# Layer 1's position bias prepared in layer 0's up stage instead of its down stage, and a cast of the down stage put behind three copies

## The chip, the cores and the metric

The kernel runs on one core of a Trainium2 chip. The metric is the device time of one launch in microseconds (us), as the median of several runs; lower is better. A hardware profile of one execution shows when each engine worked: TensorE (PE, with its weight loads PEld), VectorE (DVE), ScalarE (ACT), GpSimd (POOL), and the queues from which SyncE (SP), ACT and POOL issue transfers.

## The reference

One inference step of a two-layer encoder over 1024 new frames and 8 running streams of 16 frames, all in float32. Layer 0 uses sliding-window attention with a distance penalty, layer 1 attention over 9 chunks of 64 with a learned bias per head on the clipped relative distance. Behind each attention comes a squared-ReLU MLP:

```python
def relpos_bias(q_pos, k_pos, table):          # layer 1 only; table is rel_bias_b[0], 16 heads x 257
    rel = jnp.clip(q_pos[:, None] - k_pos[None, :], -MAX_REL, MAX_REL) + MAX_REL
    bias = table.astype(jnp.float32)[:, rel]
    return jnp.where(band_mask(q_pos, k_pos, LEFT_CHUNKS_B)[None], bias, NEG)

def mlp(x, g_norm, w_up, w_down):              # 1024 -> 4096 -> 1024
    return jnp.square(jax.nn.relu(rmsnorm(x, g_norm) @ w_up)) @ w_down
```

## The kernel before

Each layer runs four stages one after the other: attention, the output projection, the **up stage** (`mlp_up`) and the **down stage** (`mlp_down`). Every float32 operand is split into a high part (a cast, on ACT, line 128) and a low part (source minus high, on DVE, line 134), and every product of two tiles is three matmuls (`mm3`, lines 745 to 747).

The up stage walks over 16 blocks `b` of 256 hidden columns. `weights(b)` loads two raw tiles `ru` through SP's queue (three buffers), forms differences on DVE and splits them into `wq` and `w`. `tokens` runs seven products per block into the PSUM tiles `ps_x`, `ps_y`, `ps_z`; ACT copies or activates them (lines 866, 871, 875, 818, 819) and DVE adds them (868, 877, 886) into the tiles `h` (seven buffers, taken in turn). Block 0 does this in two halves of 256 tokens. POOL then stores sums of `h` to DRAM (`hd`, line 910).

The down stage multiplies in 40 products per layer, two rounds of 20 (`RANK`). Product `n` needs one tile `a` of rows (768 KB, loaded from `hd` through SP's queue, line 1026, three buffers, loaded as soon as the product that used the buffer is done) and one weight tile `w` (from the raw tiles `r`, or from their sum `s`, line 1062). Both are split first: `split_h` and `split_w`. A product is three groups of 12 matmuls, one for each of three PSUM banks `ps_c`. Products come in chains that go on accumulating into the same three banks; between two products of a chain some outputs read the banks, either as a copy to `o` by ACT (line 1165), or as an addition into `x` by DVE (line 1177). The copies `o` are added to DRAM by POOL's transfers.

In layer 0's down stage two functions prepare the bias of layer 1. `prep_bias`, ahead of product 20, loads the table `tb`, fills `fr` and `big` on DVE, turns the table into `fr`, writes it to DRAM (`fd`) and repeats it there 128 times (`rd`, 3 MB). `spread_bias`, ahead of product 24, reads 16 pieces of `rd` into `big` and stores that to DRAM (`biasSd`). All 20 transfers go through SP's queue, at places that `self.behind` (an order without a semaphore) sets behind the loads issued so far.

The order on each engine is set by a scheduler that simulates the program, by the hand-set orders of `self.behind`, `self.follow` (TensorE) and `chain` (DVE), and by priorities.

Of the kernel before, what the change touches and what calls it, by code (L numbers as in the profile page):

```python
# [8 lines left out]
F32 = mybir.dt.float32  # L9
F32R = mybir.dt.float32r  # L10
AF = mybir.ActivationFunctionType
ALU = mybir.AluOpType
# [4 lines left out]
P = 128  # L17
# [5 lines left out]
H = 16  # L23
KV = 4
G = 4
# [5 lines left out]
RANK = 20  # L31
# [21 lines left out]
BIG = 1e30  # L53
NREL = 257
# [40 lines left out]
class Build:  # L95
# [681 lines left out]
    def mlp_up(self, layer, sx, x8, rp, raw0):  # L777
        nc = self.nc
        tt = nc.vector.tensor_tensor
        with ExitStack() as st:  # L780
# [113 lines left out]
            self.pe = None  # L894
            for b in range(NFB):
                quad, ws = weights(b)
                eh = [hp.tile([P, 3 * 3 * P], F32, tag="h", name="h", bufs=7) for _ in range(2)]
                if b == 0:
                    tokens(eh, quad, ws, slice(0, 256), False)
                    tokens(eh, quad, ws, slice(256, 512), True)  # L900
                else:
                    tokens(eh, quad, ws, slice(0, 512), True)
                if b % 2 == 0:
                    even = eh
                    self.forms_even(b // 2, eh)
                else:
                    self.forms_odd(b // 2, even + eh, hp.tile([P, 3 * 3 * P], F32, tag="h", name="ht", bufs=7))
# [59 lines left out]
    def mlp_down(self, layer, out):  # L967
# [3 lines left out]
        with ExitStack() as st:  # L971
# [15 lines left out]
            for n, tags in enumerate(DOWN_HOME):  # L987
                pool = self.pool(st, f"d{n}_{layer}")
                for t in tags.split():
                    if t == "bias":  # L990
                        self.bias_tiles(pool)
                        pool.tile([P, 248], F32, tag="pad", name="pad")
                    elif t[0] == "+":
                        pool.tile([P, int(t[1:])], F32, tag="gap", name="gap")
                    else:
                        homes[t] = pool
                        slots[t] = fresh(t)
# [71 lines left out]
            def split_h(n):  # L1069
                if n < total:  # L1070
                    a = aa[n]
                    low[n] = [self.split(a[:, 0], a[:, 1], a[:, 1].bitcast(F32))[1]]

            low, total_of = {}, {}
            banks = None
# [48 lines left out]
                    chain(z)  # L1124
            late = iter(self.late)
            for n, (s, p, g, first, final, reads, _) in enumerate(seq):
                if layer == 0 and n == RANK:
                    self.prep_bias(self.dp)
                if layer == 0 and n == RANK + 4:
                    self.spread_bias(self.dp)  # L1130
                if n + AHEAD < total:
                    load_w(n + AHEAD)
                split_h(n + 1)
# [17 lines left out]
                for i in range(3):  # L1151
                    if i == 2 and n + 2 in total_of:
                        chain(total_of[n + 2])
                    c = slice(i * P, i * P + P)
                    z = [
                        self.mm3(
                            banks[i], a[:, 0, k, c], a[:, 1, k, c], w[:, 0, k], w[:, 1, k],
                            first and k == 0, k == 3,
                        )
                        for k in range(4)  # L1160
                    ]
                    self.follow(z[0][0], z[-1][1])
                    for o, v in reads:
                        if o in adds:
                            nc.scalar.activation(adds[o][i], banks[i], AF.Copy, scale=float(v))  # L1165
# [11 lines left out]
                        chain(tt(x, x, banks[i], ALU.add if v > 0 else ALU.subtract))  # L1177
                    for o in {o // 2: o for o, _ in reads if left[o] == n}.values():
                        store_x(o, PARTS[o // 2][i])
# [10 lines left out]
                            break  # L1190
                        load_h(m)

    def bias_tiles(self, pool):
        self.tb = pool.tile([H, NREL], F32, tag="tb", name="tb")
        self.fr = pool.tile([H, 384], F32, tag="fr", name="fr")
        self.big = pool.tile([P, KV, 288], F32, tag="big", name="big")

    def prep_bias(self, dp):
        nc = self.nc
        with ExitStack() as st:  # L1200
            tb, fr, big = self.tb, self.fr, self.big
            a = nc.sync.dma_start(tb, self.ins["rel_bias_b"][0])
            self.behind(self.sp, a)
            self.behind(self.dve, nc.vector.memset(fr, 0.0))
            self.behind(self.dve, nc.vector.memset(big, BIG))
            nc.vector.tensor_scalar(
                fr[:, 127:383], tb[:, 256:0:-1], -1.0, tb[:, 256:257], ALU.mult, ALU.add
            )
            fd = dp.tile([H, 384], F32, tag="fd", name="fd")
            nc.sync.dma_start(fd, fr)  # L1210
            rd = dp.tile([H, P, 384], F32, tag="rd", name="rd")
            nc.sync.dma_start(rd, fd[0:H].unsqueeze(1).to_broadcast([H, P, 384]))
            ra = rd[0:H]

            def fsrc(h, off, n, nh, hs, w):
                return bass.AP(
                    tensor=ra.tensor, offset=ra.offset + h * P * 384 + 127 + off,
                    ap=[[383, n], [hs * P * 384, nh], [1, w]],
                )

            self.fsrc = fsrc

    def spread_bias(self, dp):
        nc, big, fsrc = self.nc, self.big, self.fsrc
        for h4 in range(G):
            for b in range(2):
                r = slice(h4 * 32 + b * 16, h4 * 32 + b * 16 + 16)
                c = 256 + b * 16
                for z in (
                    nc.sync.dma_start(big[r, :, b * P : b * P + P], fsrc(h4, 0, 16, KV, G, P)),  # L1230
                    nc.sync.dma_start(big[r, :, c : c + 16], fsrc(h4, P, 16, KV, G, 16)),
                ):
                    self.behind(self.sp, z)
        self.biasSd = dp.tile([KV, P, 288], F32, tag="biasSd", name="biasSd")
        nc.sync.dma_start(self.biasSd[0:KV].rearrange("j p c -> p j c"), big)

    def prep_gains(self):
        nc, I = self.nc, self.ins
# [593 lines left out]
def make_plan(tail, second):  # L1832
# [16 lines left out]
AFTER = mybir.DependencyInfo(mybir.DependencyClass.NoSync, mybir.DependencyReason.DATA)  # L1849
EARLY = (300, 150, 110, 90)  # L1850
DOWN_HOME = (
    "s1", "r0", "o0", "+512", "s0", "o1", "+512", "r3", "x5", "x6", "x7", "bias", "r4", "r5", "+384", "x8", "x0", "x2", "+640",
    "a0", "x1", "x3", "x4", "r6", "a1", "a2", "w0", "w1", "r7", "r8", "r9", "r10",
)
TAIL = 6
# [56 lines left out]
```

## Time and profile before

| | |
|---|---|
| runs | 2354.15, 2354.36, 2357.34 us; median 2354.36 us |
| span of the profiled execution, first to last instruction | 2349.6 us (its own time is not given beside it) |
| TensorE busy | 2273.2 us, 97% of the span |
| DVE, ACT, POOL busy | 73%, 57%, 27% |
| layer 0's up stage, about | 426 to 798 us |
| layer 0's down stage, about | 798 to 1133 us |
| layer 1's up stage, about | 1655 to 2017 us |
| layer 1's down stage, about | 2017 to 2346 us |

In lines of the timeline the first number is the start in us from the start of the span, the second the duration in us; then come engine, line, operation, output<-input with shape and type, and in brackets the idle time of the engine ahead of it and what ended it. A row `SPq` or `POOLq` is the issue of a transfer, not the transfer. In tables of waits the three numbers are the sum in us, how often, and the longest. In tables of windows the columns are the stretch, its length, the busy time (and count) of PE, PEld, DVE, ACT and POOL, the granted TensorE clock, the busy share of the DMA engines and GB/s.

### The profile page before, as it was taken

To read this page: it belongs to the slowest core of one execution; us is meant where nothing else is said; L and a number is where in the kernel's file an instruction comes from. 1 tells how busy PE (TensorE), PEld (TensorE's weight loads), DVE (VectorE), ACT (ScalarE), POOL (GpSimd) and SP (SyncE) were. 2 spreads that over 40 slices of the span, in tenths; PEclk is the share of its full clock that TensorE was granted. 3 is DMA by queue.
4 is the path that set the end of the run, shared out by engine and by line. 5 is a ranking of instruction groups with operands and counts; after the bars stand their busy time and mean duration, and the time that the engine had idled before them with its cause. 6 is when DMAs were issued, how large, how long until landed. Compare 5 with 4: busy or idle time off the path is not lost.

```text
span 2349.6 us, 33397 instructions
## 1 busy us (share of the span) xinstructions
PE 2273.2 (97%) x11429; PEld 1899.3 (81%) x11429; DVE 1718.3 (73%) x3075; ACT 1332.0 (57%) x2684; POOL 644.7 (27%) x950
## 2 busy tenths in 40 slices
PE   8999999899999999999899899999899999999999
PEld 6787877788888888778778778887888888888887
DVE  6888786766656578898577776877666566678987
ACT  3777674555555555344377666665655555555443
POOL 4434332313213111002433444345132132210011
PEclk9999999999999999999999999999999999999999
DMA  7435546234334687848654656555243343877567
GB/s 262 128 103 177 166 141 208 89 122 162 132 112 152 218 231 174 272 142 206 191 157 114 190 151 180 166 172 186 72 162 132 114 160 113 276 212 197 183 165 198
DMA packets 226715, 392.70 MB, mean 167 GB/s; under 512 B 51592, under 2 KB 126288, under 8 KB 226448
## 3 DMA queue, kind: packets, MB, share of 16 engines
q1 hardware_dynamic: 188816, 283.58, 37.8%
q0 software_dynamic: 36432, 102.26, 16.0%
q10 hardware_dynamic: 1296, 4.72, 0.5%
q8 instruction: 90, 1.47, 0.3%
q14 instruction: 81, 0.66, 0.1%
HBM read 236.51 MB, written 156.85 MB: 167 GB/s over the span
## 4 chain that ended last, share of the span: by engine, by line
PE 73%; DVE 11%; DMA 8%; ACT 3%; issue 2%; POOL 2%; SPq 1%; ACTq 0%; DVEq 0%; POOLq 0%
PE ps_c L745 7%; PE ps_c L746 7%; PE ps_c L747 7%; PE ps_x L745 5%; PE ps_x L747 5%; PE ps_x L746 5%; PE ps_mm L219 3%; PE ps_mm L221 3%; PE ps_mm L220 3%; PE ps_y L747 2%; PE ps_y L746 2%; PE ps_y L745 2%; PE ps_tr L326 2%; DMA a<-hd 2%; DVE w L134 1%
## 5 line engine op out<-in xcount | busy, mean ns | idle before, releaser
L746 PE MATMUL ps_c<-w,a 128*128 128x512 f32 x960 | 374.0, 390 | 3.9 <-DVE w L134 3.9
L745 PE MATMUL ps_c<-w,a 128*128 128x512 f32 x960 | 374.1, 390 | 3.2 <-ACT o L1165 1.7
L747 PE MATMUL ps_c<-w,a 128*128 128x512 f32 x960 | 373.5, 389 | 0.0
L910 POOL DMA_DIRECT2D hd<-h x272 | 149.4, 552 | 594.3 <-ACT h L819 378.4
L745 PEld LDWEIGHTS ps_c<-w,a 128*128 128x128 f32 x960 | 180.2, 188 | 42.9 <-issue 2.7
L746 PEld LDWEIGHTS ps_c<-w,a 128*128 128x128 f32 x960 | 180.2, 188 | 42.7 <-DVE w L134 5.6
L747 PEld LDWEIGHTS ps_c<-w,a 128*128 128x128 f32 x960 | 180.2, 188 | 37.4
L128 ACT CAST a<-a 128x1536 fp32r<-128x1536 f32 x80 | 118.6, 1483 | 154.6 <-DMA a<-hd 154.6
L219 PE MATMUL ps_mm<-w,hh 128*128 128x512 f32 x432 | 173.9, 403 | 12.8 <-ACT hh L128 5.4
L221 PE MATMUL ps_mm<-w,hl 128*128 128x512 f32 x432 | 172.4, 399 | 1.4 <-DVE hl L134 1.2
L220 PE MATMUL ps_mm<-w,hh 128*128 128x512 f32 x432 | 171.4, 397 | 0.3
L134 DVE TENSOR_TENSOR a<-a 128x1536 fp32r<-128x1536 f32 x80 | 140.6, 1757 | 40.6 <-ACT a L128 40.5
L745 PE MATMUL ps_x<-sx,w 128*128 128x512 f32 (+1 forms) x408 | 157.8, 387 | 4.5 <-ACT h L866 2.7
L128 ACT CAST w<-ru 128x512 fp32r<-128x512 f32 (+1 forms) x160 | 109.9, 708 | 84.4 <-PE ps_y L746 32.0
L128 ACT CAST w<-s 128x2048 fp32r<-128x2048 f32 x56 | 107.1, 1912 | 88.2 <-DVE s L1062 78.8
L747 PE MATMUL ps_x<-sx,w 128*128 128x512 f32 (+1 forms) x408 | 154.2, 378 | 0.3 <-DVE w L134 0.3
L746 PE MATMUL ps_x<-sx,w 128*128 128x512 f32 (+1 forms) x408 | 154.1, 378 | 0.0
L134 DVE TENSOR_TENSOR w<-s,w 128x2048 fp32r<-128x2048 f32 x56 | 128.2, 2289 | 32.3 <-ACT w L128 32.0
L1182 POOL DMA_DIRECT2D xp<-o x28 | 36.2, 1294 | 411.6 <-ACT o L1165 391.0
L134 DVE TENSOR_TENSOR w<-ru,w 128x512 fp32r<-128x512 f32 (+1 forms) x160 | 129.7, 813 | 14.8 <-ACT w L128 14.7
L134 DVE TENSOR_TENSOR ptl<-ps_tr,pth 128x512 fp32r<-128x512 f32 x180 | 122.5, 685 | 21.2 <-ACT pth L128 17.5
L818 ACT ACTIVATE h<-h 128x512 f32<-128x512 f32 (+1 forms) x102 | 61.9, 607 | 122.1 <-DVE h L868 93.0
(274 smaller groups left out, 6152.9 us busy)
## 6 DMA issues: line engine op xcount, KB each, us to landing
a<-hd SPq DMA_DIRECT2D x80, 768.0 KB, 6.2
hd<-h POOLq DMA_DIRECT2D x272, 192.0 KB, 2.5
ru<-in_w_up SPq DMA_DIRECT2D x64, 512.0 KB, 3.9
r<-in_w_down SPq DMA_DIRECT2D x32, 1024.0 KB, 9.8
xp<-o POOLq DMA_DIRECT2D x28, 768.0 KB, 9.5
o<-oTd SPq DMA_DIRECT2D x50, 256.0 KB, 3.9
x<-xp SPq DMA_DIRECT2D x23, 512.0 KB, 5.5
xp<-xo SPq DMA_DIRECT2D x18, 512.0 KB, 2.9
```

Of the source, the lines that this page charges most:

```text
L128: a = nc.scalar.copy(hi, src)
L134: return a, e.tensor_tensor(lo, src, hi.bitcast(F32), ALU.subtract)
L219: nc.tensor.matmul(ps, a, w[:, 0, k, :], start=(k == 0), stop=False)
L220: nc.tensor.matmul(ps, a, w[:, 1, k, :], start=False, stop=False)
L221: self.lp = nc.tensor.matmul(ps, b, w[:, 0, k, :], start=False, stop=(k == KC - 1))
L326: self.lp = nc.tensor.transpose(pt[:, i, :], get(i), self.ident)
L745: a = mm(ps, ah, bh, start=first, stop=False, skip_group_check=True)
L746: mm(ps, ah, bl, start=False, stop=False, skip_group_check=True)
L747: return a, mm(ps, al, bh, start=False, stop=last, skip_group_check=True)
L818: a = nc.scalar.activation(t, src, AF.Relu)
L910: return lambda p, z: self.nc.gpsimd.dma_start(self.hd[c // 4][:, p, c % 4], z)
L1182: nc.gpsimd.dma_start(dst, z, accum_op=ALU.add)
```

## The change

The bias of layer 1 is now prepared in layer 0's up stage, between `weights(0)` and the first block's products, in one function. Its two tiles are the first two buffers of `h`: `part` holds `tb` and `fr`, and `big` the 16 pieces. All its transfers but one are issued by POOL; `rd` is still issued by SP. In the down stage of both layers the place of the bias tiles is left as a gap of the same size, and the cast of product 2's rows is ordered behind the last of the copies `o` that read product 0's banks (`self.copied`).

```diff
@@ mlp_up
                 quad, ws = weights(b)
+                if layer == 0 and b == 0:
+                    part, big = [hp.tile([P, 3 * 3 * P], F32, tag="h", name="hb", bufs=7) for _ in range(2)]
+                    self.spread_bias(self.dp, part, big)
                 eh = [hp.tile([P, 3 * 3 * P], F32, tag="h", name="h", bufs=7) for _ in range(2)]
@@ mlp_down
-                    low[n] = [self.split(a[:, 0], a[:, 1], a[:, 1].bitcast(F32))[1]]
+                    z = self.split(a[:, 0], a[:, 1], a[:, 1].bitcast(F32))
+                    if n == 2:
+                        self.behind(self.copied, z[0])
+                    low[n] = [z[1]]
...
-                if layer == 0 and n == RANK:
-                    self.prep_bias(self.dp)
-                if layer == 0 and n == RANK + 4:
-                    self.spread_bias(self.dp)
...
-                            nc.scalar.activation(adds[o][i], banks[i], AF.Copy, scale=float(v))
+                            self.copied = nc.scalar.activation(
+                                adds[o][i], banks[i], AF.Copy, scale=float(v)
+                            )
@@ bias
-    def bias_tiles(self, pool):
...
-    def prep_bias(self, dp):
...
+    def spread_bias(self, dp, part, big):
+        nc = self.nc
+        dma = nc.gpsimd.dma_start
+        tb, fr = part[0:H, 0:NREL], part[0:H, 384:768]
+        dma(tb, self.ins["rel_bias_b"][0])
+        nc.vector.memset(fr, 0.0)
+        nc.vector.memset(big, BIG)
+        nc.vector.tensor_scalar(
+            fr[:, 127:383], tb[:, 256:0:-1], -1.0, tb[:, 256:257], ALU.mult, ALU.add
+        )
+        fd = dp.tile([H, 384], F32, tag="fd", name="fd")
+        dma(fd, fr)
+        rd = dp.tile([H, P, 384], F32, tag="rd", name="rd")
+        nc.sync.dma_start(rd, fd[0:H].unsqueeze(1).to_broadcast([H, P, 384]))
...
+        big = big.rearrange("p (j c) -> p j c", j=KV)
         for h4 in range(G):
             for b in range(2):
...
-                    nc.sync.dma_start(big[r, :, b * P : b * P + P], fsrc(h4, 0, 16, KV, G, P)),
-                    nc.sync.dma_start(big[r, :, c : c + 16], fsrc(h4, P, 16, KV, G, 16)),
...
+                dma(big[r, :, b * P : b * P + P], fsrc(h4, 0, 16, KV, G, P))
+                dma(big[r, :, c : c + 16], fsrc(h4, P, 16, KV, G, 16))
...
-        nc.sync.dma_start(self.biasSd[0:KV].rearrange("j p c -> p j c"), big)
+        dma(self.biasSd[0:KV].rearrange("j p c -> p j c"), big)
@@ DOWN_HOME
-    ... "x7", "bias", "r4" ...
+    ... "x7", "+2048", "r4" ...
```

In the built program the lines behind the edits have other numbers (the copy to `o`, 1165 before, is 1164 now; the store of `h`, 910 before, is 913). The following rows are the order on an engine, without times.

ACT at the start of layer 0's down stage, before (the casts `a` here are the rows of products 1, 2 and 3, the casts `w` the weights of products 1 and 2; `ps_x`, `h` belong to the last block of the up stage):

```order
L128 CAST a_8973<-a_8973 128x1536
L819 ACTIVATE h<-h 128x512
L128 CAST w_9005<-s_8894 128x2048
L128 CAST a_8993<-a_8993 128x1536
L818 ACTIVATE h<-h 128x512
L819 ACTIVATE h<-h 128x512
L1165 ACTIVATE o_8902<-ps_c 128x512 x3
L128 CAST w_9086<-r_9009 128x2048
L1165 ACTIVATE o_8914<-ps_c 128x512
L128 CAST a_9081<-a_9081 128x1536
```

The same place now:

```order
L128 CAST a_8998<-a_8998 128x1536
L819 ACTIVATE h<-h 128x512
L128 CAST w_9030<-s_8922 128x2048
L818 ACTIVATE h<-h 128x512
L819 ACTIVATE h<-h 128x512
L1164 ACTIVATE o_8930<-ps_c 128x512 x3
L128 CAST a_9018<-a_9018 128x1536
L128 CAST w_9111<-r_9034 128x2048
L1164 ACTIVATE o_8942<-ps_c 128x512
L128 CAST a_9106<-a_9106 128x1536
```

The cast of product 2's rows has moved from ahead of the two activations to behind the three copies; the rest keeps its order. In layer 1 it moves the same way.

SP's queue around product 20 of layer 0's down stage, before (`hd_124` holds the rows of the second round):

```order
L1026 DMA a_10038<-hd_124 128x1536
L1202 DMA tb<-in_rel_bias_b 16x257
L1026 DMA a_10094<-hd_124 128x1536
L1210 DMA fd<-fr 16x384
L1212 DMA rd<-fd 2048x1x384
L1026 DMA a_10145<-hd_124 128x1536
L1026 DMA r_10147<-in_w_down 128x4x512
L1026 DMA a_10196<-hd_124 128x1536
```

There only the loads of `a` and `r` are left now. In SP's queue of the up stage stands, now:

```order
L662 DMA x<-xp_112 128x1024
L662 DMA x<-xp_113 128x1024
L773 DMA ru<-in_w_up 128x4x256 x2
L1207 DMA rd<-fd 2048x1x384
L773 DMA ru<-in_w_up 128x4x256 x27
```

Of the 20 transfers of the bias this one has stayed in SP's queue: it stands behind the first half of block 2's weights (`ru`) and ahead of the second half.

POOL at the start of layer 0's up stage, now (before, line 642 was followed by the stores of `h` at once):

```order
L642 TENSOR_TENSOR mrs<-mms,mhalf 128x1
L1198 DMA hb<-in_rel_bias_b 16x257
L1205 DMA fd<-hb 16x384
L1222 DMA hb<-rd 16x4x128
L1223 DMA hb<-rd 16x4x16
...
L1223 DMA hb<-rd 16x4x16
L913 DMA hd_123<-h 128x384 x5
L1225 DMA biasSd<-hb 128x4x288
L913 DMA hd_123<-h 128x384 x9
```

The sixteen pieces, which read `rd`, have moved ahead of block 0's five stores of `h`, and the store of the bias stands behind these. On DVE the two memsets stand ahead of a weight subtraction, and the operation that forms `fr` between lines 868 and 877 of block 0's first half. Beyond these places the scheduler has exchanged neighbours: in layer 1's up stage ACT's first copy of line 871 now precedes the activations of lines 818 and 819 (as it did in layer 0), and in layer 1's attention some score matmuls, transposes and their subtractions change places.

More of the change, by code (lines that the diff above doesn't have):

```diff
@@ L989, in mlp_down @@
                 for t in tags.split():
[L990 to L993, printed above, removed]
+                    if t[0] == "+":
                         pool.tile([P, int(t[1:])], F32, tag="gap", name="gap")
@@ L1191, in mlp_down, with fsrc @@
                         load_h(m)
-    def bias_tiles(self, pool):
-        self.tb = pool.tile([H, NREL], F32, tag="tb", name="tb")
-        self.fr = pool.tile([H, 384], F32, tag="fr", name="fr")
-        self.big = pool.tile([P, KV, 288], F32, tag="big", name="big")
-    def prep_bias(self, dp):
-        nc = self.nc
[L1200 to L1207, printed above, removed]
-            )
[L1209 to L1224, printed above, removed]
+    def spread_bias(self, dp, part, big):
+        nc = self.nc
+        dma = nc.gpsimd.dma_start
[10 more added lines that the diff above has]
+        nc.sync.dma_start(rd, fd[0:H].unsqueeze(1).to_broadcast([H, P, 384]))
+        ra = rd[0:H]
+        def fsrc(h, off, n, nh, hs, w):
+            return bass.AP(
+                tensor=ra.tensor, offset=ra.offset + h * P * 384 + 127 + off,
+                ap=[[383, n], [hs * P * 384, nh], [1, w]],
+            )
+        self.fsrc = fsrc
+        big = big.rearrange("p (j c) -> p j c", j=KV)
         for h4 in range(G):
@@ L1851 @@
 DOWN_HOME = (
[L1852 removed]
+    "s1", "r0", "o0", "+512", "s0", "o1", "+512", "r3", "x5", "x6", "x7", "+2048", "r4", "r5", "+384", "x8", "x0", "x2", "+640",
     "a0", "x1", "x3", "x4", "r6", "a1", "a2", "w0", "w1", "r7", "r8", "r9", "r10",
```

3 lines of the change are left out of this document (removed).

## The prediction

> **What bounds the kernel now.** I read the page first (busy shares), then the waits of TensorE by stretch, then the timeline around each wait, and last the DMA table.
>
> ```profile
> span 2349.6 us, 33397 instructions
> PE 2273.2 (97%) x11429; PEld 1899.3 (81%) x11429; DVE 1718.3 (73%) x3075; ACT 1332.0 (57%) x2684; POOL 644.7 (27%) x950
> ```
>
> TensorE is busy 97% of the span, so a wait of another engine counts only where TensorE stands still. The change touches the two down stages and the start of layer 0's up stage. Both layers run the same 40 products in the down stage, and only layer 0 also prepares the bias there, so layer 1 is a control within one trace. TensorE's waits, first in layer 0's down stage, then from layer 1's up stage to the end:
>
> ```profile
> PE ps_c L746 <- DVE w L134: 3.7, 3, 1.7
> PE ps_c L745 <- ACT o L1165: 1.4, 1, 1.4
> PE ps_c L745 <- DVE x L1177: 1.0, 2, 0.5
> ...
> PE ps_c L745 <- DVE x L1177: 0.5, 1, 0.5
> PE ps_c L745 <- ACT o L1165: 0.3, 1, 0.3
> PE ps_c L746 <- DVE w L134: 0.2, 1, 0.2
> ```
>
> Columns: sum in us, times, longest. Layer 0 waits 6.1 us, layer 1 waits 1.0 us for the same products. The timeline of TensorE gives the places; the figure in brackets is the idle time shown:
>
> ```profile
> 806.12 0.39 PE L747 MATMUL ps_c<-w,a 128*128 128x512 f32 x1
> 807.88 0.50 PE L745 MATMUL ps_c<-w,a 128*128 128x512 f32 x1 [1.38 <-ACT o L1165]
> 808.22 0.39 PE L746 MATMUL ps_c<-w,a 128*128 128x512 f32 x1
> ...
> 972.85 0.50 PE L746 MATMUL ps_c<-w,a 128*128 128x512 f32 x1 [1.06 <-DVE w L134]
> 1000.16 0.50 PE L746 MATMUL ps_c<-w,a 128*128 128x512 f32 x1 [1.74 <-DVE w L134]
> 1017.68 0.50 PE L746 MATMUL ps_c<-w,a 128*128 128x512 f32 x1 [0.91 <-DVE w L134]
> 1034.58 0.47 PE L745 MATMUL ps_c<-w,a 128*128 128x512 f32 x1 [0.51 <-DVE x L1177]
> ...
> 2025.85 0.50 PE L745 MATMUL ps_c<-w,a 128*128 128x512 f32 x1 [0.28 <-ACT o L1165]
> 2189.84 0.50 PE L746 MATMUL ps_c<-w,a 128*128 128x512 f32 x1 [0.22 <-DVE w L134]
> 2345.31 0.39 PE L747 MATMUL ps_c<-w,a 128*128 128x512 f32 x1
> ```
>
> Undisturbed matmuls start 0.227 us apart (1440 of them take 328 us in layer 1, below). Around the first wait the starts lie 1.76 and 0.34 us apart, so it costs 1.76 + 0.34 - 2 x 0.227 = 1.65 us: the idle time shown plus 0.27 us. I use that sum for each wait.
>
> **The cast behind the sum copies.** Product 1 accumulates into the three banks that product 0 filled, so it waits until ACT has copied them (L1165). In ACT's queue the cast of product 2's rows stands ahead, and it waits for its load:
>
> ```profile
> 804.67 1.48 ACT L128 CAST a<-a 128x1536 fp32r<-128x1536 f32 x1 [2.81 <-DMA a<-hd]
> ```
>
> ACT is idle for 2.81 us although two of the three banks can be full by then. With the cast last, the two activations and two copies run before 806, the third copy ends near 807, and the cast runs about 807.1 to 808.6. Who waits for it: the weights' cast behind it on ACT, which ends near 810.5 as now (the copies and the cast have only changed places), and on DVE the subtraction of the rows and then that of the weights:
>
> ```profile
> 810.63 2.29 DVE L134 TENSOR_TENSOR w<-r,w 128x2048 fp32r<-128x2048 f32 x1 [2.68 <-ACT w L128]
> ```
>
> DVE idles 2.68 us ahead of that row, which is room for the later rows, and ends at 812.9. Product 1 needs 36 x 0.227 = 8.2 us from 806.35, so product 2 starts at 814.5, 1.6 us later. So the delay of the cast is covered; without that cover it would cost up to the 2.4 us by which it moves. Gain: 1.65 us in layer 0. In layer 1 the same swap removes 0.28 + 0.27 = 0.55 us. Together 2.2 us; bounds 0 (the copies wait for something else) and 2.2.
>
> **The bias out of the down stage.** It removes two memsets and one small operation from DVE and 20 transfers from SP's queue. What hurts is a transfer of 3 MB (rd) ahead of the rows' loads in that queue:
>
> ```profile
> 976.84 0.60 SPq L1212 DMA_DIRECT2D rd<-fd  x1
> rd<-fd SPq DMA_DIRECT2D x1, 3072.0 KB, 15.7
> 994.63 1.48 ACT L128 CAST a<-a 128x1536 fp32r<-128x1536 f32 x1 [3.41 <-DMA a<-hd]
> 2202.85 1.48 ACT L128 CAST a<-a 128x1536 fp32r<-128x1536 f32 x1
> ```
>
> rd lands at 976.84 + 15.7 = 992.5, the rows behind it at 994.6. Layer 1 runs 1217.0 us behind (2189.84 - 972.85), so its cast at 2202.85 corresponds to 985.9: layer 0 is 8.7 us late, and DVE's w for the wait at 1000.16 comes after that cast. Layer 1 shows no wait there, nor at the places of 1017.68 and 1034.58 (there sixteen small transfers stand in the queue ahead of a load). I take layer 1's rows as what is left: 1.74 + 0.27 = 2.01, 0.91 + 0.27 = 1.18, 0.51 + 0.27 = 0.78. At 972.85, where DVE's memsets come ahead of the rows' subtraction, 1.06 - 0.22 = 0.84 goes. Sum 4.8 us. As a check, the stage from its first to its last matmul:
>
> ```profile
> 798.18 0.39 PE L745 MATMUL ps_c<-w,a 128*128 128x512 f32 x1
> 1132.40 0.39 PE L747 MATMUL ps_c<-w,a 128*128 128x512 f32 x1
> 2017.26 0.39 PE L745 MATMUL ps_c<-w,a 128*128 128x512 f32 x1
> ```
>
> 1132.40 - 798.18 = 334.2 us against 2345.31 - 2017.26 = 328.1: 6.1 us, of which the first cast's difference is 1.1, so 5.0 us is left for the bias. Bounds 0.8 and 5.0; layer 1 is near, so 4.8.
>
> **The bias in the up stage.** DVE gets memsets and an operation of 0.38 + 1.02 + 0.34 us:
>
> ```profile
> 967.40 0.38 DVE L1204 MEMSET fr<- 16x384 f32 x1
> 967.97 1.02 DVE L1205 MEMSET big<- 128x1152 f32 x1 [0.19 <-issue]
> 974.92 0.34 DVE L1206 TENSOR_SCALAR fr<-tb 16x256 f32<-16x256 f32 x1
> 449.20 0.42 DVE L877 TENSOR_TENSOR h<-ps_y,h 128x256 f32<-128x256 f32 x1 [3.99 <-PE ps_y L747]
> ```
>
> All three stand before L877, ahead of which DVE idles 3.99 us: it has done all else at 449.20 - 3.99 = 445.2, and would at 446.9 with 1.74 us more. So 0 us.
>
> POOL issues tb, fd, sixteen pieces and the store ahead of or among h's stores; SP issues rd behind the second block's loads. The next rows are how long h's stores from POOL take to land, and the weights' load behind rd for which ACT waits, with what follows:
>
> ```profile
> DMA to landing us min/median/max: 2.1/2.5/12.5
> 468.05 1.05 ACT L128 CAST w<-ru 128x1024 fp32r<-128x1024 f32 x1 [1.33 <-DMA ru<-in_w_up]
> 469.00 0.58 ACT L866 COPY h<-ps_x 128x512 f32<-128x512 f32 x1
> 470.44 0.39 PE L745 MATMUL ps_x<-sx,w 128*128 128x512 f32 x1
> 495.58 0.59 ACT L871 COPY h<-ps_x 128x512 f32<-128x512 f32 x1 [0.20 <-PE ps_x L747]
> ```
>
> With fr ready at 446.9, fd's issue and landing of 0.55 and 2.5 us (as h's stores) let rd go near 450 and land 15.7 later, near 465.7. Rows behind rd landed 2.1 us after it, so the weights land near 467.8, no later than now; L866 has 470.44 - 469.58 = 0.86 us to spare. rd may therefore land as late as 466.8 for nothing, and each microsecond more costs one. Sixteen pieces and five stores of h at 0.55 us each end near 477, the bias' store lands near 481; its buffer is next written by L871 at 495.58, so 14 us are to spare. I take 0 and keep 0 to 3 us for the range.
>
> **Orders that fall out of it.** In layer 1's up stage the copy L871 now precedes two activations:
>
> ```profile
> 445.95 0.39 PE L745 MATMUL ps_x<-sx,w 128*128 128x256 f32 x1 [0.54 <-ACT h L871]
> 1665.03 0.39 PE L745 MATMUL ps_x<-sx,w 128*128 128x256 f32 x1 [1.28 <-ACT h L871]
> ```
>
> Layer 0, where the copy is first already, waits 0.54; so 1.28 - 0.54 = 0.7 us goes. In layer 1's attention near 1183 to 1196 some twenty instructions change places on DVE, ACT and PE while TensorE is busy throughout: 0, with 2 us either way, about the 1.74 us of the longest single wait above. Stage changes also move against the clock:
>
> ```profile
> 1140.00:1145.00 5.00, 4.14 (x10) 3.26 (x11) 3.90 (x6) 2.15 (x4) 0.00 (x0) 0.50 0.66 170
> ```
>
> After the gap at the start of layer 1 TensorE's clock is granted at 0.50 in this stretch (the column before the last two). A half-clocked matmul lasts 0.2 us longer, so eight more or fewer of them make 1.7 us either way. [...]
>
> **Sum.** 2.2 + 4.8 + 0.7 = 7.7 us. Against the profiled span, 2349.6 - 7.7 = 2341.9. The profile gives that execution no other time; the runs' median, 2354.36, is 4.8 us above its span, which I take as what lies around it: 2346.7 us. A change of 0.2% (4.7 us) is about what a measurement can tell here.
>
> **Rivals.**
> Only part goes (chance 0.23): the w at DVE is late anyway, since ACT waits for rows in most products of layer 0, and the copies' place brings 1 to 2 us while the bias brings 1 to 2. For it: DVE is the busiest helper in that stage. Against it: layer 1's three clean places. About 3 us faster, 2351.4, no change to a measurement.
>
> rd collides in the up stage (0.07, the other side): tb or fd land late on POOL's queue. Single landings of h's stores reach 12.5 us (row above). The point that decides is rd's landing: beyond 466.8 the wait of TensorE grows one for one, since the cast stands ahead of L866 on ACT, and beyond 474.5 all 7.7 us are gone. Behind a late tb DVE also holds L877, and with it the bank of the next product. At 482, which takes a tb or fd some 16 us late, the kernel is 7 us slower, 2362. Against it: no other load is issued between the second block's and the third's, and a landing of 12.5 us is the longest of 272.
>
> POOL starves (0.03): each of its 19 issues waits for an operation of DVE and takes 2.3 us (the longest DVE row above) instead of 0.55. rd then lands near 467.5 (0.7 us of wait), the pieces, the five stores and the bias' store take 22 x 2.3 = 51 us more and land near 521, and L871 waits 25 us for its buffer: 2346.7 + 26 = 2373, slower. The row that speaks against it is 272 issues at 552 ns each, in stages where DVE works all the time:
>
> ```profile
> L910 POOL DMA_DIRECT2D hd<-h x272 | 149.4, 552 | 594.3 <-ACT h L819 378.4
> ```
>
> [...]
>
> **Chances and range.** Forecast 0.67 (5 to 10 us faster); partial gain 0.23, within 0.2%; collision 0.07, of which 0.05 slower and 0.02 near zero; starved POOL 0.03, slower. So faster 0.67, same 0.25, slower 0.08. The forecast's own range is 2344 to 2350 (2 us for the reordered attention, 1.7 for the clock); to leave out no more than 2 in 10 it reaches to 2342.5 and, through the partial gain and a short collision, to 2354.
>
> **What would show it.** After: no wait on ACT's o at product 1 in either layer; layer 0's down stage about 328 us from first to last matmul; no cast of rows late by 8 us; ACT's wait for ru near 468 within 1 us of now and TensorE unbroken at 470; L871 of layer 1 at 0.5 us. Wrong: a new wait on ru or on DVE's L877 in the first two blocks of the up stage, or waits on w near the 24th product that remain.

## The result, and the profile after

| | median (lowest to highest) | before, beside it | ratio, 95% interval |
|---|---|---|---|
| the change | 2345.45 (2339.61 to 2351.22) us, 7 runs | 2354.41 us, 7 runs | 0.9955 [0.9940, 0.9970] |
| the same kernel once more | 2343.00 (2336.18 to 2348.11) us, 8 runs | 2354.31 us, 31 runs | 0.9948 [0.9930, 0.9965] |

The change makes the kernel 0.45% faster: 10.6 us by the ratio, between 7 and 14.

```profile
span 2349.4 us, 33413 instructions
...
PE 2274.9 (97%) x11429; PEld 1900.9 (81%) x11429; DVE 1716.7 (73%) x3075; ACT 1332.6 (57%) x2684; POOL 652.6 (28%) x969
```

These are the first lines of the page after. The span is as long as before (2349.6), which seems to contradict the times. But this execution took 2351.22 us, the longest of its seven. So two spans must not be subtracted; the gain has to be read place by place. Both traces have 11429 matmuls. For each k, the start of the k-th matmul after is compared with that of the k-th before; the table says by how much this difference changes at each place. Negative is faster than before, in us. "Once more" is the second profile of the same kernel; the cast alone and the bias alone are described below.

| place (us on the scale of before) | change | once more | cast alone | bias alone | predicted |
|---|---|---|---|---|---|
| layer 0's attention and output projection, to 426 | +4.67 | +3.38 | +0.43 | +4.27 | 0 |
| its up stage, 449 to 798 | 0.00 | -0.03 | +0.03 | -0.03 | 0 |
| product 1, 807.88 | -1.68 | -1.68 | -1.68 | -0.03 | -1.65 |
| 810 to 870 | +0.40 | +0.37 | +0.97 | -0.07 | 0 |
| 972.85 | -1.35 | -0.80 | +2.40 | -0.87 | -0.84 |
| 1000.16 | -2.03 | -2.03 | +0.03 | -2.03 | -2.01 |
| 1017.68 | -1.21 | -1.21 | 0.00 | -1.21 | -1.18 |
| 1034.58 | -0.79 | -0.79 | -0.02 | -0.79 | -0.78 |
| layer 1's start and attention, 1132 to 1640 | +1.41 | -8.98 | -4.35 | +1.58 | 0 ± 2 |
| L871, 1665.03 | -0.77 | -0.65 | +0.20 | -0.77 | -0.7 |
| product 1 of layer 1, 2025.85 | -0.60 | -0.60 | -0.60 | -0.13 | -0.55 |
| 2050 to 2090 | +0.77 | 0.00 | +0.48 | +1.89 | 0 |
| 2189.84 | +0.91 | -0.18 | -0.17 | +1.36 | 0 |

The places that the change touches lost 6.4 and 7.6 us in its two profiles (the sum of the rows without the two attentions); those of the prediction alone lost 8.4 and 7.8. Layer 1's attention alone differs by 10.4 us between two executions of the same kernel, of the 15.0 us by which their spans differ (2349.4 and 2334.4); that is not the change.

Two stretches are not in the table. From 426 to 449 us, where the up stage begins, the two profiles are 0.58 and 0.07 us later than before; kernels without a bias there are 0.01 to 3.41 us later. From 1640 to 1665 us both are 1.97 us ahead, but so is a kernel that still has the bias in the down stage (rd from ACT, below, 1.67 us), and the bias alone is not (+0.04), so this stretch can't be put down to the change.

Product 1 of layer 0 after, on ACT:

```profile
805.15 1.92 ACT L128 CAST w<-s 128x2048 fp32r<-128x2048 f32 x1 [1.73 <-DVE s L1062]
...
808.62 1.07 ACT L1164 ACTIVATE o<-ps_c 128x512 f32<-128x512 f32 x2
811.75 0.60 ACT L1164 ACTIVATE o<-ps_c 128x512 f32<-128x512 f32 x1 [2.06 <-PE ps_c L747]
812.24 1.47 ACT L128 CAST a<-a 128x1536 fp32r<-128x1536 f32 x1
813.61 1.91 ACT L128 CAST w<-r 128x2048 fp32r<-128x2048 f32 x1
```

Two copies run right behind the activations, the third as soon as its bank is full, and the cast comes behind it; ACT is idle here for no load. TensorE's waits of layer 0's down stage, and below the dots those of layer 1's:

```profile
PE ps_c L745 <- DVE x L1178: 0.3, 1, 0.3
PE ps_c L745 <- ACT o L1164: 0.3, 1, 0.3
...
PE ps_c L746 <- DVE w L134: 1.1, 1, 1.1
PE ps_c L745 <- DVE x L1178: 0.5, 1, 0.5
PE ps_c L745 <- ACT o L1164: 0.4, 1, 0.4
```

Of 6.1 us in layer 0, 0.6 us is left; layer 1 has 2.0 us in this execution, where it had 1.0. The up stage that took the bias in (SP, POOL, ACT):

```profile
454.19 0.59 SPq L1207 DMA_DIRECT2D rd<-fd  x1
...
452.45 0.49 POOL L1205 DMA_DIRECT2D fd<-hb  x1 [4.01 <-DVE hb L1201]
467.34 0.53 POOL L1222 DMA_DIRECT2D hb<-rd  x1 [14.40 <-ACT w L128]
...
473.34 1.05 ACT L128 CAST w<-ru 128x1024 fp32r<-128x1024 f32 x1 [1.43 <-DMA ru<-in_w_up]
474.30 0.58 ACT L866 COPY h<-ps_x 128x512 f32<-128x512 f32 x1
```

This execution lies 5.25 us later there (4.67 from the table and 0.58 at the start of the stage). The cast of `ru` at 473.34 is then at 468.1 on the scale of before, where it stood at 468.05; its wait was 1.33 us and is 1.43. The load it waits for goes out at 469.03, 463.8 on the scale of before, and it went out at 463.83 before. rd took 12.5 us here, so it had landed near 461.4 on that scale: this load was never behind it.

### The profile page after: what moved, and what is told of

Same layout as the page of the kernel before. It is cut to its first block, busy times and chain, and to the rows that moved or that the text cites. A ratio compares the mean times of both kernels' runs of the same rounds, so it can differ in the third digit from the quotient of the medians.

```text
span 2349.4 us, 33413 instructions
## 1 busy us (share of the span) xinstructions
PE 2274.9 (97%) x11429; PEld 1900.9 (81%) x11429; DVE 1716.7 (73%) x3075; ACT 1332.6 (57%) x2684; POOL 652.6 (28%) x969
## 4 chain that ended last, share of the span: by engine, by line
PE 76%; DVE 9%; DMA 6%; issue 4%; ACT 3%; POOL 1%; SPq 0%; POOLq 0%; ACTq 0%; DVEq 0%
PE ps_c L745 7%; PE ps_c L746 7%; PE ps_c L747 7%; PE ps_x L745 5%; PE ps_x L747 5%; PE ps_x L746 5%; PE ps_mm L219 4%; PE ps_mm L221 4%; PE ps_mm L220 3%; PE ps_y L747 2%; PE ps_y L745 2%; PE ps_y L746 2%; PE ps_tr L326 2%; PE ps_mm L176 2%; PE ps_mm L177 1%
```

## The experiments

The theory says that there are two gains that add up (the cast's place; the bias' 3 MB and memsets out of the down stage), and that the up stage hides the bias. "Places" below are those of the table. A ratio is to the kernel before, timed in the same comparison. Diffs are shortened: `...` stands for what is left out.

**The cast alone**, on the kernel before:

```diff
-                    low[n] = [self.split(...)[1]]
+                    z = self.split(...)
+                    if n == 2: self.behind(self.copied, z[0])
+                    low[n] = [z[1]]
...
-                            nc.scalar.activation(adds[o][i], ...)
+                            self.copied = nc.scalar.activation(adds[o][i], ...)
```

> Only the cast order is changed; the bias stays in layer 0's down stage. Theory (two gains that add up): product 1 of layer 0 loses its wait for ACT's copies (1.6 us), that of layer 1 0.45 us, and about 0.4 us comes back a few products later in each layer, so about 1.3 us faster than before, near 2353; the waits on DVE's w at 972.85, 1000.16, 1017.68 and 1034.58 stay (sum of idle time 3.7 and 0.5 us). Rival (the cast's place and the bias wait on the same late chain): the w waits shrink too, and the kernel gains 3 us or more, 2351 or less.

Measured: 2353.96 us, ratio 0.9995 [0.9980, 1.0009]. Product 1 gained 1.68 and 0.60 us; the three later waits stayed to 0.03 us. At 972.85 it lost 2.40 us, which neither expectation had:

```profile
974.51 0.39 PE L745 MATMUL ps_c<-w,a 128*128 128x512 f32 x1
976.71 0.50 PE L746 MATMUL ps_c<-w,a 128*128 128x512 f32 x1 [1.81 <-DVE w L134]
...
978.35 0.63 PE L746 MATMUL ps_c<-w,a 128*128 128x512 f32 x1
...
976.00:980.00 4.00, 3.29 (x10) 2.65 (x11) 4.00 (x4) 1.03 (x1) 0.00 (x0) 0.75 0.50 181
```

The wait is 0.75 us longer here than before (1.81 against 1.06), and 1.3 us after it the matmuls lengthen from 0.39 to 0.63 us and start 0.43 instead of 0.23 us apart; the window shows a granted clock of 0.75. So 1.6 us of this place is a stretch at half clock.

**The bias alone**: the changed kernel, with

```diff
-                    if n == 2: self.behind(self.copied, z[0])
```

> Only the bias is moved; the cast of product 2's rows stays ahead of the copies. Theory: the four w waits of layer 0's down stage go (5.65 us) and L871 of layer 1 loses 0.8 us, product 1's wait of 1.38 us stays: 6 to 6.5 us faster than before, near 2348, and 1.5 to 2.5 us slower than the full change. Rival (only part goes without the cast's order): w waits of 1 us or more remain near the 24th product, 2351 to 2352.

Measured: 2348.19 us, ratio 0.9979 [0.9963, 0.9994]. The three waits are gone to the hundredth of the full change, product 1 keeps its wait (-0.03). At these places the two parts are independent, as the theory said. By places it gained 2.7 us, less than the full change by 1.65 us at product 1 and 0.47 in layer 1; what else it lacks stands in the rows at 2050 and 2189, which differ between two executions of one program (below).

**No bias at all**: `spread_bias` keeps one memset and the store, and `fsrc`, which layer 1's loads use, reads the weights:

```diff
-        dma(tb, ...); nc.vector.memset(fr, 0.0); nc.vector.tensor_scalar(fr, ...)
-        dma(fd, fr); nc.sync.dma_start(rd, ...)
-        ra = rd[0:H]
+        ra = self.ins["w_up"]
-                dma(big[...], fsrc(...))    # sixteen
```

> The full change, but the bias is not prepared at all: tb, fr, fd, rd and the sixteen pieces are left out (one memset of big and its store remain), and layer 1 loads as many bytes from the weights in place of rd. Theory (the up stage hides all of the bias): the same time as the full change within 0.2%, the stretch from 440 to 800 us as long as there within 0.3 us. Rival (the bias costs 0 to 3 us in the up stage): faster than the full change by what it costs, 1 us or more, seen as a step near 450 to 500 us.

Measured: 2347.55 us, ratio 0.9971 [0.9954, 0.9989]; 449 to 798 us: +0.03 against 0.00 with the bias. In the up stage the bias costs nothing that TensorE shows. By the times it is no faster than with the bias (2345.45 and 2343.00 us; the intervals overlap). At 972.85 it waits 1.77 us, where the change waited 0 and 0.2 us: for that wait neither a memset nor the bias' transfers are needed.

**The changed kernel once more.**

> The changed kernel unchanged, for a second profile and more times. Theory: median 2345 to 2346, single times spread over some 10 us with the granted clock; all steps at the places of the change as in the first profile (product 1 of layer 0 without wait, about 0.4 us of wait on ACT's o some products later, no w waits in layer 0's down stage). If the wait of 1.1 us on DVE's w at product 20 of layer 1 belongs to the program, it is there again at 0.8 to 1.4 us; if it is chance, it is 0.5 or less. The 3.7 us by which layer 0's attention was longer in the first profile than before the change should be 1 us or less if it was chance.

Measured: the second line of the first table. The wait at 2189.84 is chance: +0.91, then -0.18, with the same program; so is the copy's wait at 2050 to 2090. Layer 0's attention, which the change does not touch, was long again (+3.38), but within 1 us of before in five of the kernels below and above (+0.43 with the cast alone). Most of it is granted clock (the column before the last two). Two stretches before, and the same in the first profile after:

```profile
20.00:35.00 15.00, 13.79 (x65) 11.16 (x64) 8.99 (x17) 2.69 (x6) 7.23 (x10) 1.00 1.00 372
65.00:80.00 15.00, 13.48 (x77) 10.93 (x75) 11.57 (x42) 10.56 (x33) 6.30 (x13) 1.00 0.44 154
...
20.00:35.00 15.00, 12.18 (x52) 9.70 (x51) 8.33 (x15) 3.17 (x8) 5.86 (x8) 0.89 0.98 347
65.00:80.00 15.00, 13.48 (x65) 10.64 (x64) 11.04 (x42) 9.19 (x29) 5.93 (x13) 0.89 0.41 138
```

A clock of 0.89 over 15 us is worth about 1.65 us, so these two stretches make an estimated 3.3 of the 4.67 us.

**rd from ACT's queue**, still in the down stage of the kernel before:

```diff
-            nc.sync.dma_start(rd, fd[0:H]...)
+            nc.scalar.dma_start(rd, fd[0:H]...)
```

> The kernel before with one issue moved: rd (3 MB) is still written at the same place of layer 0's down stage, but from ACT's queue instead of SP's. Theory (rd costs by standing ahead of the rows' loads in SP's queue): the cast of rows at 994.63 comes near 986 to 989, the wait of 1.74 us at 1000.16 goes (2.0 us), those at 1017.68 and 1034.58 (1.2 and 0.8 us) stay; ACT's wait for fd ahead of the issue may cost up to 2 us of ACT but no TensorE time. About 2 us faster than before. Rival (rd costs by its bytes, whatever its queue): the cast is still 5 us or more late, at 991 or later, and the wait at 1000.16 stays at 1 us or more.

Measured: 2353.58 us, ratio 0.9989 [0.9977, 1.0002]. Each theory got half. 1000.16 gained 1.62 of 2.03 us, but the cast of rows is still late. The row load that it needs and the cast, first before (its cast at 994.63 is in the prediction), then here:

```profile
981.15 0.33 SPq L1026 DMA_DIRECT2D a<-hd  x1
...
984.73 0.33 SPq L1026 DMA_DIRECT2D a<-hd  x1
996.59 1.48 ACT L128 CAST a<-a 128x1536 fp32r<-128x1536 f32 x1 [1.78 <-DMA a<-hd]
...
rd<-fd ACTq DMA_DIRECT2D x1, 3072.0 KB, 18.9
```

From the load's issue to the cast it is 13.5 us behind rd and 11.9 us beside it. Out of the queue, rd gives back 1.6 us; the rest comes with its bytes. The column before the last is the busy share of the DMA engines while this load is on its way, first here, then in the kernel without rd (below):

```profile
989.00:993.00 4.00, 3.81 (x17) 2.82 (x15) 4.00 (x3) 0.64 (x2) 0.00 (x0) 1.00 0.95 271
...
981.00:985.00 4.00, 4.00 (x20) 3.30 (x19) 4.00 (x5) 1.22 (x1) 0.00 (x0) 1.00 0.76 259
```

Beside rd the engines are busy 0.95 of the window, without it 0.76. The load takes 11.9 us beside rd and at most 4.7 without it, and rd itself slows from 15.7 to 18.9 us. How the engines share their time between the two queues is not shown.

**The pieces from POOL**, rd still on SP:

```diff
-                for z in (nc.sync.dma_start(big[...], fsrc(...)), nc.sync.dma_start(big[...], fsrc(...))):
-                    self.behind(self.sp, z)
+                nc.gpsimd.dma_start(big[...], fsrc(...))
+                nc.gpsimd.dma_start(big[...], fsrc(...))
-        nc.sync.dma_start(self.biasSd...
+        nc.gpsimd.dma_start(self.biasSd...
```

> The kernel before with the sixteen pieces of rd and the bias' store issued by POOL instead of SP, still in the down stage; rd stays on SP. Theory (each transfer costs by its place in SP's queue ahead of rows' loads): the waits at 1017.68 and 1034.58 (1.2 and 0.8 us) go, those at 972.85 and 1000.16 stay; about 2 us faster than before. Rival (these two waits are the echo of rd, whose late rows the following products inherit): each keeps 0.5 us or more.

**Both** of the last two diffs, all in the down stage.

> The kernel before with rd on ACT's queue and the pieces and the store on POOL's: the bias stays in the down stage, but nothing of 3 MB and no piece stands in SP's queue. Theory (the queue, not the stage): of the 4.0 us at 1000.16, 1017.68 and 1034.58 at least 3.4 go, 972.85 stays (memsets on DVE): 3.4 to 4 us faster than before. Rival (the down stage is the wrong place whatever the queue, by bandwidth or by ACT's and POOL's own time): 2 us or more of waits remain there or come up elsewhere between 970 and 1050.

**Without rd**, the pieces still on SP:

```diff
-            nc.sync.dma_start(rd, fd[0:H]...)
-            ra = rd[0:H]
+            ra = self.ins["w_up"]
```

> The kernel before without rd: the transfer of 3 MB is left out, and what reads rd (the sixteen pieces, still on SP in the down stage, and layer 1's loads) reads as many bytes of the weights. Memsets, tb, fd, pieces and store stay where they were. Theory after the runs with rd on ACT's and the pieces on POOL's queue (rd costs by its bytes: the row load beside it takes 11.8 us from either queue, and DVE, idle for that row, has a backlog until 1035): without the bytes all three waits at 1000.16, 1017.68 and 1034.58 go (4.0 us), the row load issued near 981 lands in 4 to 6 us, and the wait at 972.85 stays at 0.8 us or more; 4 us faster than before. Rival (the pieces in SP's queue make the last two): 2.0 us remain at 1017.68 and 1034.58.

| | ratio, interval | 972.85 | 1000.16 | 1017.68 | 1034.58 |
|---|---|---|---|---|---|
| rd from ACT | 0.9989 [0.9977, 1.0002] | +0.71 | -1.62 | -0.01 | -0.01 |
| pieces from POOL | 1.0002 [0.9990, 1.0013] | +0.49 | +1.85 | -1.21 | -0.45 |
| both | 0.9988 [0.9973, 1.0003] | +0.23 | -1.59 | -0.01 | -0.03 |
| without rd | 0.9969 [0.9954, 0.9983] | -0.21 | -2.03 | -1.21 | -0.79 |

The pieces' place is worth nothing: "both" stands within 0.03 us of "rd from ACT" at the three places. With the pieces on POOL and rd on SP the three sum to +0.19: at 1000.16 a half-clock stretch followed the wait (1.94 us idle; clock 0.71 from 1002 to 1006 us), and TensorE, later by 1.85 us, waited less at the next two (that the one made the other is an argument, not a measurement). Without rd's bytes all three go, with the pieces still in SP's queue; by the times that kernel is 4 to 11 us faster than before. What carries the last two waits is DVE, here in "both":

```profile
999.88 1.76 DVE L134 TENSOR_TENSOR a<-a 128x1536 fp32r<-128x1536 f32 x1 [3.72 <-ACT a L128]
...
1014.01 2.28 DVE L1062 TENSOR_TENSOR s<-r,r 128x2048 f32<-128x2048 f32 x1
...
1019.08 2.28 DVE L134 TENSOR_TENSOR w<-s,w 128x2048 fp32r<-128x2048 f32 x1
...
1021.42 0.50 PE L746 MATMUL ps_c<-w,a 128*128 128x512 f32 x1 [0.91 <-DVE w L134]
```

DVE idles 3.72 us for the late rows, and from 999.88 to 1025 its rows show no idle time: it works off a backlog, and the weights' subtraction at 1019.08 comes too late. Without rd:

```profile
980.88 0.32 SPq L1026 DMA_DIRECT2D a<-hd  x1
...
985.60 1.48 ACT L128 CAST a<-a 128x1536 fp32r<-128x1536 f32 x1
...
PE ps_c L746 <- DVE w L134: 0.8, 1, 0.8
PE ps_c L745 <- DVE x L1177: 0.5, 1, 0.5
```

The row load takes at most 4.7 us, and of TensorE's waits between 960 and 1050 only 972.85 and one of 0.5 us are left. The rows' cast now also stands ahead of the weights' cast in ACT's order, as in the changed kernel, since the scheduler no longer counts rd. So it is not shown how much of the gain is the bytes and how much this order; the load's time, from 11.9 to 4.7 us, is the bytes. By an estimate the old order would have been enough at 1000.16: behind the weights' cast of the kernel before, which ends at 991.2, the rows' cast would still run 3.4 us earlier than at 994.63, and the wait there costs 2.0 us.

**The memsets on POOL**, in the kernel before:

```diff
-            self.behind(self.dve, nc.vector.memset(fr, 0.0))
-            self.behind(self.dve, nc.vector.memset(big, BIG))
+            self.behind(self.dve, nc.gpsimd.memset(fr, 0.0))
+            self.behind(self.dve, nc.gpsimd.memset(big, BIG))
```

> The kernel before with the two memsets of the bias (fr and big) on POOL instead of DVE; nothing else is edited. Theory (DVE's 1.5 us of memsets ahead of the rows' subtraction make the wait at 972.85): that wait falls from 1.06 to 0.2 to 0.3 us of idle time, 0.8 to 1.4 us gained there, and the three later waits stay. Rival (the row casts are late there anyway): 972.85 keeps 0.8 us or more. In time: 0.8 to 1.4 us faster, too little to tell by the runs, so the profile decides.

Measured: 972.85 gained 1.11 us, as the theory said. But the three later places lost 1.05, 5.98 and 3.39 us, and the kernel is slower, ratio 1.0027 [1.0012, 1.0042]: the scheduler, with DVE's 1.4 us of memsets gone, put three casts of rows on ACT ahead of the casts of weights that they followed. The first and what came of it:

```profile
1019.64 1.48 ACT L128 CAST a<-a 128x1536 fp32r<-128x1536 f32 x1 [7.32 <-DMA a<-hd]
1021.03 1.89 ACT L128 CAST w<-s 128x2048 fp32r<-128x2048 f32 x1
...
1022.97 0.49 PE L745 MATMUL ps_c<-w,a 128*128 128x512 f32 x1 [2.37 <-ACT w L128]
```

A cast of rows that are not there yet stands ahead of the cast of weights for which TensorE waits. It is the same kind of fault as the one that the first part of the change mends.

**All transfers of the bias from SP** in the up stage:

```diff
-        dma = nc.gpsimd.dma_start
+        dma = nc.sync.dma_start
```

> The changed kernel with all transfers of the bias in the up stage issued by SP instead of POOL. The sixteen pieces must wait for rd, and behind them in SP's queue stand the loads of the third block's weights. Theory (SP's order counts, as in the down stage): these loads are issued only when rd has landed (near 467) and the pieces are through (16 x 0.45 = 7 us), so near 474 instead of 454, TensorE waits for the third block near 495 for little or nothing if they land in 4 to 8 us, and 5 to 15 us if the pieces wait for one another; 0 to 10 us slower than the full change. Rival (the queue does not matter): within 0.3 us of the full change from 440 to 560 us.

Measured: 2344.71 us (4 runs), ratio 0.9949 [0.9930, 0.9967], 449 to 798 us: +0.02. The third block's loads went out at 469.01, and ACT was idle 3.23 us for them, at no cost, for the scheduler had put the copy L866 ahead of the cast:

```profile
469.01 0.97 SPq L773 DMA_DIRECT2D ru<-in_w_up  x2
...
470.69 0.59 ACT L866 COPY h<-ps_x 128x512 f32<-128x512 f32 x1 [1.27 <-PE ps_x L747]
474.50 1.05 ACT L128 CAST w<-ru 128x1024 fp32r<-128x1024 f32 x1 [3.23 <-DMA ru<-in_w_up]
```

POOL's queue is not needed. At 972.85 this execution waits 1.41 us, without any memset on DVE there: the rows' cast ahead of it waited 5.19 us for its load, where it waited 3.29 before.

**rd twice**: 3 MB more in SP's queue, in the up stage of the changed kernel:

```diff
+        r2 = dp.tile([H, P, 384], F32, tag="r2", name="r2")
+        nc.sync.dma_start(r2, fd[0:H]...)
         nc.sync.dma_start(rd, fd[0:H]...)
```

> The changed kernel with a second copy of rd (3 MB more) issued by SP ahead of rd in the up stage. Theory (rd may land as late as 466.8 on the scale of the first profile of before, each microsecond beyond costs one): with 12.5 us for the first 3 MB the second lands near 474 on that scale, so TensorE waits about 7 to 12 us near 470, and the kernel is that much slower than the full change. Rival (transfers overlap, and the weights' loads behind rd get their share): rd and ru land together within 5 us more than now, and TensorE waits less than 3 us.

Measured: 2348.46 us, ratio 0.9962 [0.9948, 0.9976]; 449 to 500 us: +4.62, between the two expectations.

```profile
rd<-fd SPq DMA_DIRECT2D x1, 3072.0 KB, 26.3
...
477.10 1.04 ACT L128 CAST w<-ru 128x1024 fp32r<-128x1024 f32 x1 [4.60 <-DMA ru<-in_w_up]
478.05 0.58 ACT L871 COPY h<-ps_x 128x512 f32<-128x512 f32 x1
...
478.68 0.50 PE L745 MATMUL ps_x<-sx,w 128*128 128x512 f32 x1 [2.72 <-ACT h L871]
```

rd landed 9 us later than the limit of the prediction, and TensorE waited 2.72 us for L871, the copy behind the cast, plus 1.6 us of half clock (clock 0.65 from 478 to 482 us). L866 had again been put ahead.

**A third buffer for `o`** in the gap that the bias tiles left:

```diff
-    ... "x7", "+2048", "r4" ...
+    ... "x7", "o2", "+512", "r4" ...
-                        z = take(f"o{no % 2}")
+                        z = take(f"o{no % (3 if n > 2 else 2)}")
```

> The changed kernel with a third buffer for the copies o, in the gap that the bias tiles left in the down stage; used from product 3 on. Theory (the small wait that came up after the change, 0.2 to 1.0 us between 830 and 870 us and 0 to 1.9 us between 2050 and 2090 us, is ACT's copy waiting until POOL's transfer has emptied its buffer): both stretches end 0.2 us or less above those of before. Rival (something else holds the copy, as the bank or the casts ahead of it): they stay at 0.2 to 1.0 us in at least one layer. In time at most 1 us faster than the full change, too little to tell by the runs; the profile decides.

Measured: 2350.63 us, ratio 0.9980 [0.9968, 0.9993]. The change had 0.9955 and 0.9948, so this kernel is the slower one, though its interval just touches that of the first comparison (up to 0.9970). 830 to 870: +3.82; 2050 to 2090: +6.48. The remedy fails, again through ACT's order. Since by its simulation a buffer is free, the scheduler put a product's copies behind the next rows' and weights' casts:

```profile
837.02 1.49 ACT L128 CAST a<-a 128x1536 fp32r<-128x1536 f32 x1 [2.64 <-DMA a<-hd]
839.01 1.92 ACT L128 CAST w<-s 128x2048 fp32r<-128x2048 f32 x1 [0.51 <-DVE s L1062]
846.18 2.06 ACT L1164 ACTIVATE o<-ps_c 128x512 f32<-128x512 f32 x4 [5.26 <-DMA xp<-o]
...
848.30 0.55 PE L745 MATMUL ps_c<-w,a 128*128 128x512 f32 x1 [2.12 <-ACT o L1164]
```

Order and buffer changed together, so this run does not test the theory. The traces do name the wait: in the change's first profile TensorE waits for a copy that ACT holds until POOL's transfer has emptied its buffer. The same copy before, then after, and TensorE's wait for it:

```profile
839.45 0.60 ACT L1165 ACTIVATE o<-ps_c 128x512 f32<-128x512 f32 x1 [3.39 <-DMA xp<-o]
...
843.97 0.60 ACT L1164 ACTIVATE o<-ps_c 128x512 f32<-128x512 f32 x1 [5.21 <-DMA xp<-o]
...
844.62 0.50 PE L745 MATMUL ps_c<-w,a 128*128 128x512 f32 x1 [0.27 <-ACT o L1164]
```

Why the buffer comes free later with the cast moved stays open. No version beat the change; the one with all on SP equals it.

## Why the prediction was right, point by point

- **The cast behind the copies**: 1.65 and 0.55 us predicted, 1.68 and 0.60 measured, in every kernel that had it. That its own delay is covered held at product 2. Not foreseen: 0.4 to 2.1 us comes back between 810 and 870 in five of six executions with the cast moved (0.40 and 0.37 in the change itself, -0.17 with all on SP), against -0.17 to +0.15 in the six kernels with the cast where it was. So the cast's place gives some of its gain back, in the first profile by the wait for `o` shown above; the prediction put nothing for it.
- **The bias out of the down stage**: 4.8 us predicted, 5.4 and 4.8 measured at the four places (0.84 was 1.35 and 0.80; 2.01, 1.18 and 0.78 were 2.03, 1.21 and 0.79). Taking layer 1 as the control gave these to 0.03 us. The step that failed is the reason: "What hurts is a transfer of 3 MB (rd) ahead of the rows' loads in that queue", and sixteen small ones ahead of a load. The queue is worth 1.6 of 4.0 us, the pieces none; without the bytes, and with the order on ACT that came with that, all of it goes. The sum did not depend on which, since both left the stage together: there the number was right for a reason that was not.
- **The wait at 972.85**: the prediction took the memsets for its cause. On DVE they matter only on top of a late row load: the idle time lay between 0 and 1.77 us among the kernels without memsets there. That the change waited only 0 and 0.2 us in its two profiles, so that 0.84 came true as 1.35 and 0.80, is in part luck.
- **The up stage**: 0 predicted, 0.00 and -0.03 measured, and the kernel without a bias agrees. The cast of `ru` was forecast within 1 us of 468 and is at 468.1. The way there was another: rd was to land near 465.7 with the weights 2.1 us behind it, but it landed near 461.4, and the weights' load, which goes out only at 463.8, no longer had it ahead.
- **L871 of layer 1**: 0.7 predicted, 0.77 and 0.65 measured.
- **The clock**: that eight matmuls more or fewer run at half clock was the author's estimate, and no run shows it as a bound; with the cast alone one such stretch cost 1.6 us. 1.7 us either way was too little for single executions: the two profiles of one kernel differ by 10.4 us in layer 1's start and attention. From 1125 to 1150, 1330 to 1345 and 1545 to 1560 us the granted clock is 0.86, 0.89 and 0.89 in the first and 0.93, 1.00 and 1.00 in the second, which makes an estimated 5 us of it; the rest was not taken apart.
- **The time around the span**: 4.8 us was wrong as named. Each execution of the changed kernel takes 1.8 us more than its span; the profiled one of before was thus probably 3 us faster than the median. The forecast did not suffer, since it amounts to the median less 7.7 us.
- **Sum**: 7.7 us predicted; by places 6.4 and 7.6, by the medians 9 and 11 (the first interval begins at 7). 2346.7 forecast, 2345.45 measured. No run here assigns the 2.6 and 3.7 us by which the medians exceed the places: layer 1's attention, where some twenty instructions changed their order, spreads by more than that between executions.
- **Rivals**: "Only part goes" fell at the three places. "rd collides" can happen but was priced too high: from 466.8 on, each microsecond was to cost one. In the run with rd twice, rd landed 9 us beyond that and the kernel paid 2.7 us of wait and 1.6 us of clock, since the copy L866 no longer stood behind the cast. "POOL starves" has no trace: the sixteen issues took 0.51 us each, in 467 to 475 us.

## What to carry to other kernels

When two stages run the same work and only one carries an extra, the clean one is the best estimate of what is left once the extra is gone; it was right to 0.03 us where the reasoning about queues was not. Moving a large transfer to another queue gave back only 1.6 of 4.0 us to the loads that share its bandwidth: move it to a time when nobody waits for a load. And in an engine's fixed order, work that waits for a load must not stand ahead of work for which TensorE waits; after each edit look at that order again, for an edit elsewhere (a memset, a spare buffer) can turn it around and cost more than it saves.

## What the runs showed of the hardware

- Two nearly equal waits differed by 1.6 us in what followed: 1.81 us of idle time of TensorE (cast alone, 976.71) and 1.77 us (no bias, 981.15). Of the single idle times named here, those of 1.81 us, 1.94 (pieces from POOL), 2.12 (third buffer), 2.30 and 2.37 (memsets on POOL) and 2.72 us (rd twice) were followed by a stretch at half clock; those of 1.38 and 1.74 us (before, 807.88 and 1000.16) and of 1.77 us were not, and neither was this one, with the memsets on POOL:

```profile
1004.21 0.50 PE L746 MATMUL ps_c<-w,a 128*128 128x512 f32 x1 [2.79 <-DVE w L134]
...
1006.00:1012.00 6.00, 6.00 (x28) 4.99 (x27) 6.00 (x5) 3.08 (x2) 0.00 (x0) 1.00 0.30 95
```

  In the kernel with the cast alone the long matmuls run from 978.0 to 981.3, 3.4 us. The length of the idle time alone does not sort these rows, for 2.79 us cost no half clock and 1.81 us did; what decides is not shown.
- The same 768 KB load took 4.7 us or less without the 3 MB transfer, 11.9 us beside it in another queue and 13.5 us behind it in its own.
